# Quarter sums on GpSimd ahead of the convolution, and the convolution's norm among V's tiles

## Chip, core and metric

The kernel runs on one core of one Trainium2 chip. What counts is the device time of one execution in microseconds. The core has five engines with a queue each: PE (TensorE, matmuls), DVE (VectorE), ACT (ScalarE), POOL (GpSimd) and SP (SyncE, which here only issues DMAs; POOL issues some too). Each takes its instructions in a fixed order and waits on semaphores for the others.

## What is computed

One layer of a streaming encoder over 1040 tokens (16 learned ones and 1024 of input) of width 1024: three token mixers on the normalised input, gated, added and projected, and then a hierarchical mixture of experts. Cut to what matters here:

```python
def conv_module(bv, bg, conv_w, conv_b, ln_g, ln_b):
    glu = bv * jax.nn.sigmoid(bg)
    y = causal depthwise convolution of glu with 31 taps, 256 channels
    y = layer_norm(y + conv_b, ln_g, ln_b)      # (y - mu) * rsqrt(var + EPS)
    return jax.nn.silu(y)

def mixer_layer(u, w_in, ...):
    a, bv, bg, q, k, v, fg, gates = split(u @ w_in)
    ya = pool_mixer(a, ...) @ w_out_a
    yb = conv_module(bv, bg, ...) @ w_out_b
    logf = jax.nn.log_sigmoid(fg + b_forget)
    yc = forgetting_attention(heads(q), heads(k), heads(v), logf) @ w_out_c
    g = jax.nn.sigmoid(gates)                   # three branches of 1024 each
    return (g[0] * ya + g[1] * yb + g[2] * yc) @ w_o
```

## The kernel before

**Precision.** Matmuls work on values that are split in two: a rounded part ("hi", made by ACT, L171) and the remainder ("lo", made by DVE or POOL as raw minus hi, L172). A product is three matmuls: hi by hi, hi by lo, lo by hi. The normalised input u lies transposed in four slots, hi and lo for each half of its channels (`u4`); `uq(part, r, c)` is a quarter of the real tokens' part of it: channel half r, token half c, 128 partitions x 4 x 512 = 128x2048 values.

**Order of the work.** The projections are jobs that run one after another on PE: the convolution's gate and value, the pool mixer's input, then K (four jobs, matmuls L177, evictions L290 and L291 into a ring of eight buffers, copies to DRAM by POOL's queue at L292 and L293), V (nine tiles of 128 tokens, two halves each, matmuls L587; a tile's values are split from PSUM, L171 and L172, into the same slot as K's ring, and copied to DRAM at L595), the forget gate (L605 to L627), and two jobs of Q. V's weights come in four blocks of 128x1040, each split on ACT and DVE.

The vector work of the mixers doesn't stand in jobs. `start_b` fills a list, `pending`, in the order pool mixer, convolution, sums; each job takes some entries from its head when it is emitted (`pump(n)`): 13 for each K job, 3 for each tile of V, 4 for each Q job, and all that is left (`pump(1000)`) at the start of `seven`. The convolution's entries are 62 taps on DVE (L455, L457: accumulator plus input times weight, 128x1024 each), then its norm: `ln_sum` and `ln_mean` (mean over channels by PE with a matrix of ones, L471, and DVE, L484), `ln_var` (variance, square root on ACT at L497, reciprocal on DVE at L498, one Newton step L499 to L502), `ln_out` for each half (L506 to L510), `ln_free`, and the spill of yb to DRAM (`dy`), which frees its slot.

**Sums and products.** The rest of Q and the three gates, 13 column pairs, are computed in `seven` by seven half-size products for each pair instead of eight (a scheme of Strassen's kind; L680, 1092 matmuls of 512 columns). Its right sides are quarters of u and four sums of quarters: x = u01 - u00 (kept in place of u01 at the end, L639, L640), `tq[3]` = u11 - u01, `tq[2]` = u11 - x, `tq[4]` = u10 - tq[2]'s sum, each added over its hi and lo parts in two scratch halves x and y of slot `s_wx`, and split again (L545, L546). Its left sides are sums of weight blocks, made by POOL (L659 to L662) in the halves of the same slot `s_wx`, then split. The results go to DRAM as `dq` and `dg`. Attention, the projections out and the experts follow.

Within a stage the order of the instructions on each engine is set when the program is built: by the order of the code, as far as what an instruction needs is ready by then.

Of the kernel before, what the change touches and what calls it, by code (L numbers as in the profile page):

```python
# [8 lines left out]
F32R = mybir.dt.float32r  # L9
BF16 = mybir.dt.bfloat16  # L10
I32 = mybir.dt.int32
AF = mybir.ActivationFunctionType
# [29 lines left out]
def view(a, off, shape, dt=None):  # L42

    n = 1
    for s in shape:
        n *= s
    a = a[:, off:off + n]
    if dt is not None:
        a = a.bitcast(dt)
    if len(shape) == 2:  # L50
        a = a.rearrange("p (a b) -> p a b", b=shape[1])
    elif len(shape) == 3:
        a = a.rearrange("p (a b c) -> p a b c", b=shape[1], c=shape[2])
    return a
# [63 lines left out]
def f32(ap):  # L118
    return ap.bitcast(F32)


def body(tc, A, out):
# [3 lines left out]
    with es:  # L126
# [171 lines left out]
        def pump(n):  # L298
            for _ in range(min(n, len(pending))):
                pending.pop(0)()  # L300
# [91 lines left out]
        def start_b(_):  # L392
            s_x.free(), s_un.free()
            nonlocal qk_r
            s_qk, s_acc, s_ya = sl.take(F32R), sl.take(), sl.take(F32R)
            st["s_qk"], st["s_acc"], st["s_ya"] = s_qk, s_acc, s_ya
            qk_r = s_qk.ring(512, 8)
            st["acc"], st["sq"] = s_acc.new([2, S]), s_acc.new([2, S])
            st["yaT"] = s_ya.new([2, 2, S])
            queue_pool()  # L400
            queue_conv()
            queue_sums()

        job(lambda: None, start_b)

# [42 lines left out]
        def queue_conv():  # L448
            acc = st["acc"]

            def tap(k, ct):
                src = glu[:, ct, k:k + S]
                wk = cvec[:, 31 * ct + k:31 * ct + k + 1]
                if k == 0:
                    ve.tensor_scalar(acc[:, ct, :], src, wk, vec("conv_b", ct), ALU.mult, ALU.add)  # L455
                else:
                    ve.scalar_tensor_tensor(acc[:, ct, :], src, wk, acc[:, ct, :], ALU.mult, ALU.add)  # L457
            for k in range(31):
                for ct in range(2):
                    pending.append(lambda k=k, ct=ct: tap(k, ct))  # L460

            def both(x, ct):

                yb = st["ybT"]
                t = st["sq"][:, ct, :]
                ve.tensor_add(t, x[:, 0, :], x[:, 1, :])
                split(t, yb[:, 0, ct, :], yb[:, 1, ct, :])

            def over_channels(o, ct, cs):
                for part in range(2):  # L470
                    pe.matmul(o, ones, st["ybT"][:, part, ct, cs], start=part == 0, stop=part == 1)  # L471

            def ln_sum():
                st["s_yb"] = sl.take(F32R)
                st["ybT"] = st["s_yb"].new([2, 2, S])
                both(acc, 0)

            def ln_mean():
                for c in range(2):
                    o = mm_bk.next()  # L480
                    cs = slice(c * 512, c * 512 + 512)
                    over_channels(o, 0, cs)
                    for ct in range(2):
                        ve.scalar_tensor_tensor(acc[:, ct, cs], o, -1.0 / 256, acc[:, ct, cs], ALU.mult, ALU.add)  # L484
                        ac.activation(st["sq"][:, ct, cs], acc[:, ct, cs], AF.Square)

            def ln_var():
                vr, rs = sg_r.next([L])[:, 0:S], sg_r.next([L])[:, 0:S]
                st["rs"] = rs
                both(st["sq"], 1)  # L490
                for c in range(2):
                    o = mm_bk.next()
                    cs = slice(c * 512, c * 512 + 512)
                    over_channels(o, 1, cs)
                    ve.tensor_scalar(vr[:, cs], o, 1.0 / 256, EPS, ALU.mult, ALU.add)

                ac.activation(rs, vr, AF.Sqrt)  # L497
                ve.reciprocal(rs, rs)  # L498
                ve.tensor_mul(vr, vr, rs)  # L499
                ve.tensor_mul(vr, vr, rs)  # L500
                ve.tensor_scalar(vr, vr, -0.5, 1.5, ALU.mult, ALU.add)
                ve.tensor_mul(rs, rs, vr)  # L502

            def ln_out(ct):
                z, sq = acc[:, ct, :], st["sq"][:, ct, :]
                ve.tensor_mul(z, z, st["rs"])  # L506
                ve.tensor_scalar(z, z, vec("conv_ln_g", ct), vec("conv_ln_b", ct), ALU.mult, ALU.add)
                ac.activation(sq, z, AF.Sigmoid)
                ve.tensor_mul(sq, z, sq)
                yb = st["ybT"]  # L510
                split(sq, yb[:, 0, ct, :], yb[:, 1, ct, :])

            def ln_free():
                st["s_acc"].free(), s_glu.free()
            pending.extend([ln_sum, ln_mean, ln_var, lambda: ln_out(0), lambda: ln_out(1), ln_free,
                            lambda: spill(1, "yb")])

# [3 lines left out]
        def uq(part, r, c):  # L521
            return u4[2 * part + r][:, :, M + c * 512:M + c * 512 + 512]

        def queue_sums():
            def begin():
                st["s_t"] = [sl.take(F32R) for _ in range(3)]
                st["s_wx"] = sl.take()
                for n, x in zip((2, 3, 4), st["s_t"]):
                    tq[n] = [x.new([4, 512]) for _ in range(2)]
                st["x"], st["y"] = (view(st["s_wx"].ap, o, [4, 512]) for o in (2048, 0))  # L530
            pending.append(begin)

            def diff(to, r1, c1, r0, c0, other):

                return [lambda: ve.tensor_sub(st[to], f32(uq(0, r1, c1)), f32(uq(0, r0, c0))),
                        lambda: ve.tensor_sub(st[other], f32(uq(1, r1, c1)), f32(uq(1, r0, c0))),
                        lambda: ve.tensor_add(st[to], st[to], st[other])]

            def less(to, r, c, of):

                return [lambda: ve.tensor_sub(st[to], f32(uq(0, r, c)), st[of]),
                        lambda: ve.tensor_add(st[to], st[to], f32(uq(1, r, c)))]

            def parts(n, of):
                return [lambda: ac.copy(tq[n][0], st[of]),  # L545
                        lambda: ve.tensor_sub(tq[n][1], st[of], f32(tq[n][0]))]  # L546
            pending.extend(diff("x", 1, 1, 0, 1, "y") + parts(3, "x") + diff("x", 0, 1, 0, 0, "y") +
                           less("y", 1, 1, "x") + parts(2, "y") + less("y", 1, 0, "y") + parts(4, "y"))

        def qk_job(col, hp, which, n, look=2):  # L550
            def comp(w):
# [5 lines left out]
            job(lambda: win_unit(col + hp * P), comp, look)  # L557

        for hp in range(4):
            qk_job(COL_K, hp, 0, 13)  # L560


        def start_v(_):
# [9 lines left out]
        def v_all(ws):  # L573

            for j in range(9):
# [17 lines left out]
                        ve.tensor_add(st["lf"][:m, :, j], o[:, 252:260], bfb[:m, :])  # L593
                if j < 8:
                    gp.dma_start(dv[j * P:(j + 1) * P, :], f32(v.rearrange("p h t d -> p (h t d)")))  # L595
                pump(3)

        job(lambda: [win_unit(COL_V + half * 260, 260, k0, k0 + 4) for half in range(2) for k0 in (0, 4)], v_all, 1)

# [1143 lines left out]
```

## Time and profile before

| | us |
|---|---|
| device time, median of 3 runs | 1220.85 (1216.33 to 1223.65) |
| device time of the profiled execution | 1217.87 |
| its span | 1216.2 |
| PE busy in the span | 1059.8 (87%) |
| DVE busy | 804.1 (66%) |
| ACT busy | 517.2 (43%) |
| POOL busy | 398.2 (33%) |

PE is the engine to follow: where it is idle, the span grows. The page's slices show where in the span that is, and the timeline of PE, with what ended each idle time, shows what it waited for there. The rows of the other engines in the same stretch then show why the thing waited for was late.

### The profile page before, as it was taken

How to read it: one execution, taken by the hardware profiler on the slowest of the kernel's cores; microseconds unless marked ns; L12 is line 12 of the kernel's file. 1: busy time of each engine (PE TensorE's matmuls, PEld its weight loads, DVE VectorE, ACT ScalarE, POOL GpSimd, SP SyncE). 2: the span in 40 equal slices, each digit the busy share in tenths (PEclk: the TensorE clock that was granted, in tenths of full speed). 3: DMA queues.
4: the chain of work that ended last, by engine and by line, in shares of the span. 5: the costliest groups of instructions: out<-in, count | busy, mean ns of one | idle time of the engine just before them, and what ended most of it. 6: DMA issues, size and time to landing. Idle time of an engine off the chain costs nothing. (4 is left out here: it accounts for less than half of the span.)

```text
span 1216.2 us, 16197 instructions
## 1 busy us (share of the span) xinstructions
PE 1059.8 (87%) x5429; PEld 883.2 (73%) x5429; DVE 804.1 (66%) x1383; ACT 517.2 (43%) x943; POOL 398.2 (33%) x459
## 2 busy tenths in 40 slices
PE   5999999614999999998999999899976889889683
PEld 5999998413788888877888888777755667767562
DVE  5799956785443443326888885467778765567864
ACT  5312225222443444436888731222324544445552
POOL 4001210323333231112333138400015664454664
PEclk9999999856999999998999999999987899999995
DMA  7413522301423233187996557243557896696974
GB/s 216 119 54 116 181 97 95 143 0 34 156 87 122 97 120 114 60 251 191 243 300 141 197 158 235 102 157 139 179 192 232 284 322 184 164 301 175 293 244 150
DMA packets 95191, 202.10 MB, mean 166 GB/s; under 512 B 11730, under 2 KB 51747, under 8 KB 94549
## 3 DMA queue, kind: packets, MB, share of 16 engines
q1 hardware_dynamic: 83844, 167.83, 43.0%
q0 software_dynamic: 10784, 31.13, 9.1%
q10 hardware_dynamic: 432, 1.57, 0.4%
q8 instruction: 60, 0.98, 0.3%
q14 instruction: 71, 0.57, 0.1%
HBM read 148.94 MB, written 58.30 MB: 170 GB/s over the span
## 5 line engine op out<-in xcount | busy, mean ns | idle before, releaser
L680 PE MATMUL ps<-slot,slot 128*128 128x512 f32 x1092 | 264.0, 404 | 54.3 <-ACT slot L171 46.1
L172 DVE TENSOR_TENSOR slot<-slot,slot 128x512 fp32r<-128x512 f32 (+3 forms) x227 | 233.6, 1048 | 117.0 <-ACT slot L171 112.0
L680 PEld LDWEIGHTS ps<-slot,slot 128*128 128x128 f32 x1092 | 211.0, 194 | 106.6 <-ACT slot L171 47.1
L171 ACT CAST slot<-slot 128x512 fp32r<-128x512 f32 (+3 forms) x244 | 188.0, 797 | 218.4 <-PE ps L177 77.0
L177 PE MATMUL ps<-slot,slot 128*128 128x512 f32 (+3 forms) x1200 | 228.0, 350 | 2.1 <-ACT slot L251 1.2
L177 PEld LDWEIGHTS ps<-slot,slot 128*128 128x128 f32 x1200 | 204.1, 189 | 22.8 <-ACT slot L251 1.7
L1422 PE MATMUL ps<-slot,slot 128*128 128x512 f32 x552 | 141.0, 411 | 19.0 <-PEq L1704 10.5
L1422 PEld LDWEIGHTS ps<-slot,slot 128*128 128x128 f32 x552 | 107.7, 198 | 50.1 <-issue 16.8
L172 DVE TENSOR_TENSOR slot<-ps,slot 128x512 fp32r<-128x512 f32 (+6 forms) x166 | 84.8, 533 | 28.5 <-ACT slot L171 27.6
L1189 PE MATMUL ps<-slot,slot 128*128 128x512 f32 x384 | 99.5, 405 | 3.8 <-ACT slot L171 3.8
L177 PE MATMUL ps<-slot,sm 128*128 128x512 f32 x276 | 81.2, 443 | 24.2 <-DVE sm L1438 22.8
L171 ACT CAST slot<-ps 128x512 fp32r<-128x512 f32 (+6 forms) x166 | 74.3, 464 | 54.1 <-PE ps L587 27.5
L177 PEld LDWEIGHTS ps<-slot,sm 128*128 128x128 f32 x276 | 55.1, 210 | 40.4 <-DVE sm L1438 27.0
L1189 PEld LDWEIGHTS ps<-slot,slot 128*128 128x128 f32 x384 | 69.9, 191 | 16.7 <-ACT slot L171 3.9
L172 POOL TENSOR_TENSOR slot<-slot,slot 128x1024 fp32r<-128x1024 f32 x32 | 79.5, 2506 | 1.0 <-ACT slot L171 0.5
L457 DVE SCALAR_TENSOR_TENSOR slot<-slot,c,slot 128x1024 f32<-128x1024 f32 x60 | 75.3, 1280 | 0.5
L659 POOL TENSOR_TENSOR slot<-slot 128x512 f32<-128x512 f32 x13 | 18.7, 1437 | 166.5 <-DMA slot<-in_w_in_dram 126.1
L817 DVE CUSTOM_DVE_ANT_0 slot<-ps,slot 128x656 f32<-128x656 f32 (+7 forms) x64 | 49.3, 771 | 24.5 <-PE ps L812 17.5
L872 PE MATMUL ps<-const,slot 128*128 128x128 f32 x352 | 60.4, 283 | 1.5 <-DVE slot L172 1.2
L689 DVE TENSOR_TENSOR slot<-ps,slot 128x512 f32<-128x512 f32 x39 | 27.0, 691 | 51.6 <-PE ps L680 29.6
L947 POOL TENSOR_TENSOR slot<-slot,slot 128x512 f32<-128x512 f32 x32 | 47.3, 1502 | 38.3 <-DVE slot L946 32.8
L182 POOL TENSOR_SCALAR stats<-stats 128x1 f32<-128x1 f32 (+1 forms) x24 | 17.5, 728 | 115.2 <-ACT slot L181 114.4
(287 smaller groups left out, 1493.7 us busy)
## 6 DMA issues: line engine op xcount, KB each, us to landing
slot<-in_exp_w_dram SPq DMA_DIRECT2D x96, 512.0 KB
slot<-in_w_in_dram SPq DMA_DIRECT2D x13, 1024.0 KB
dg<-slot SPq DMA_DIRECT2D x48, 256.0 KB
slot<-dk SPq DMA_DIRECT2D x32, 260.0 KB
slot<-in_x_dram SPq DMA_DIRECT2D x16, 512.0 KB
slot<-dg SPq DMA_DIRECT2D x16, 512.0 KB
slot<-in_w_in_dram SPq DMA_DIRECT2D x12, 512.0 KB
slot<-dF SPq DMA_DIRECT2D x8, 520.0 KB
```

What stands on the lines that cost most here:

```text
L171: ac.copy(hi, raw)
L172: (lo_eng or ve).tensor_sub(lo, raw, f32(hi))
L177: pe.matmul(o, a, b, start=i == 0, stop=i == len(ops) - 1)
L457: ve.scalar_tensor_tensor(acc[:, ct, :], src, wk, acc[:, ct, :], ALU.mult, ALU.add)
L659: gp.tensor_sub(s3, a[0, 0], a[1, 0])
L680: pe.matmul(o, x[:, k, :], y[:, k, :], start=i == 0 and m in (1, 2, 7), stop=i == 11 and m in (2, 3, 4), skip_group_check=True)
L689: ve.tensor_add(t, bank(n, m), t)
L817: ve.tensor_tensor_reduce(out=s2, in0=o, in1=n2, scale=-1.0, scalar=3.0e38, op0=ALU.add, op1=ALU.min, accum_out=mn)
L872: pe.transpose(tp[:, t * P:(t + 1) * P], p_of(g, i0 + t)[:, b * P:(b + 1) * P], ident)
L947: gp.tensor_add(m, m, t)
L1189: pe.matmul(o[:, c, :], a, b, start=n == 0, stop=n == 23)
L1422: pe.matmul(o, x[:, k, :], wk, start=q == 0 and i == 0, stop=q == 1 and i == len(ops) - 1)
```

## The change

The two first sums of quarters, x and y = tq[2]'s sum, leave the end of the list: they become five POOL operations in one entry ahead of the convolution, in a slot of their own (`s_wx` is taken there). What is left of the sums is two entries at the end of the list: `two` (splits for tq[2] and tq[4], with the two DVE sums between them) and `third` (tq[3], three DVE sums and its split), and only `third` takes the slot that yb's spill gives free. The norm's root is exp(-0.5 ln(var)) by two table functions on ACT in place of a square root on ACT and a reciprocal on DVE. Each K job takes 20 entries instead of 13, so that all entries up to `ln_var` are emitted by the end of K, and V's tiles 3 to 8 take 1, 1, 1, 2, 2 and 2: `ln_out` twice, `ln_free`, the spill with `two`, and `third`.

```diff
             queue_pool()
+            queue_sums()
             queue_conv()
-            queue_sums()
+            queue_parts()
...
-                ac.activation(rs, vr, AF.Sqrt)
-                ve.reciprocal(rs, rs)
+                ac.activation(rs, vr, AF.Ln)
+                ac.activation(rs, rs, AF.Exp, scale=-0.5)
                 ve.tensor_mul(vr, vr, rs)
...
         def queue_sums():
-            def begin():
-                st["s_t"] = [sl.take(F32R) for _ in range(3)]
+
+            def sums():
                 st["s_wx"] = sl.take()
-                for n, x in zip((2, 3, 4), st["s_t"]):
+                x, y = st["x"], st["y"] = [view(st["s_wx"].ap, o, [4, 512]) for o in (2048, 0)]
+                gp.tensor_sub(x, f32(uq(0, 0, 1)), f32(uq(0, 0, 0)))
+                gp.tensor_sub(y, f32(uq(1, 0, 1)), f32(uq(1, 0, 0)))
+                gp.tensor_add(x, x, y)
+                gp.tensor_sub(y, f32(uq(0, 1, 1)), x)
+                gp.tensor_add(y, y, f32(uq(1, 1, 1)))
+            pending.append(sums)
+
+        def queue_parts():
+            def two():
+                st["s_t"] = [sl.take(F32R) for _ in range(2)]
+                for n, x in zip((2, 4), st["s_t"]):
                     tq[n] = [x.new([4, 512]) for _ in range(2)]
...
-            pending.extend(diff("x", 1, 1, 0, 1, "y") + parts(3, "x") + diff("x", 0, 1, 0, 0, "y") +
-                           less("y", 1, 1, "x") + parts(2, "y") + less("y", 1, 0, "y") + parts(4, "y"))
+                y = st["y"]
+                for n in (2, 4):
+                    ac.copy(tq[n][0], y)
+                    ve.tensor_sub(tq[n][1], y, f32(tq[n][0]))
+                    if n == 2:
+                        ve.tensor_sub(y, f32(uq(0, 1, 0)), y)
+                        ve.tensor_add(y, y, f32(uq(1, 1, 0)))
+
+            def third():
+
+                st["s_t"].append(sl.take(F32R))
+                tq[3] = [st["s_t"][2].new([4, 512]) for _ in range(2)]
+                y = st["y"]
+                ve.tensor_sub(y, f32(uq(0, 1, 1)), f32(uq(0, 0, 1)))
+                ve.tensor_add(y, y, f32(uq(1, 1, 1)))
+                ve.tensor_sub(y, y, f32(uq(1, 0, 1)))
+                ac.copy(tq[3][0], y)
+                ve.tensor_sub(tq[3][1], y, f32(tq[3][0]))
+            pending.extend([two, third])
...
-            qk_job(COL_K, hp, 0, 13)
+            qk_job(COL_K, hp, 0, 20)
...
-                pump(3)
+                pump({3: 1, 4: 1, 5: 1, 6: 2, 7: 2, 8: 2}.get(j, 0))
```

Line numbers of the changed kernel are one higher up to the norm (L457 is L458) and twelve higher behind the sums (L587 is L599, L680 is L692).

On POOL, in the stretch of the second K job, the difference of the two orders reads so. `dk` is K in DRAM, slots 93 to 96 are the four slots of u (93 and 94 hi, 95 and 96 lo), slot 866 is `s_wx`:

```order
+L292 DMA dk<-slot_749 128x400
+L530 TENSOR_TENSOR slot_866<-slot_93 128x2048
+L531 TENSOR_TENSOR slot_866<-slot_95 128x2048
+L293 DMA dk<-slot_749 128x400
+L532 TENSOR_TENSOR slot_866<-slot_866 128x2048
+L292 DMA dk<-slot_749 128x384
+L533 TENSOR_TENSOR slot_866<-slot_94,slot_866 128x2048
+L293 DMA dk<-slot_749 128x384
+L534 TENSOR_TENSOR slot_866<-slot_866,slot_96 128x2048
 L292 DMA dk<-slot_749 128x256
 L293 DMA dk<-slot_749 128x256
```

The five sums stand between the copies of one K job, which followed one another without anything between them before.

On DVE, at the end of K and the start of V, the order before. Slot 750 is the convolution's accumulator, slot 97 its input, slots 90 to 92 are a weight block, raw, hi and lo, slot 749 is K's ring and V's buffers:

```order
L457 SCALAR_TENSOR_TENSOR slot_750<-slot_97,c_2_75,slot_750 128x1024 x3
L291 SCALAR_TENSOR_TENSOR slot_749<-ps,slot_749 128x384
L457 SCALAR_TENSOR_TENSOR slot_750<-slot_97,c_2_75,slot_750 128x1024
L291 SCALAR_TENSOR_TENSOR slot_749<-ps,slot_749 128x256
L172 TENSOR_TENSOR slot_92<-slot_90,slot_91 128x1040
L457 SCALAR_TENSOR_TENSOR slot_750<-slot_97,c_2_75,slot_750 128x1024 x2
L172 TENSOR_TENSOR slot_749<-ps,slot_749 128x4x64
```

And now:

```order
L458 SCALAR_TENSOR_TENSOR slot_750<-slot_97,c_2_75,slot_750 128x1024 x2
L291 SCALAR_TENSOR_TENSOR slot_749<-ps,slot_749 128x256
L458 SCALAR_TENSOR_TENSOR slot_750<-slot_97,c_2_75,slot_750 128x1024 x3
L172 TENSOR_TENSOR slot_92<-slot_90,slot_91 128x1040
L458 SCALAR_TENSOR_TENSOR slot_750<-slot_97,c_2_75,slot_750 128x1024
L172 TENSOR_TENSOR slot_92<-slot_90,slot_91 128x1040
L458 SCALAR_TENSOR_TENSOR slot_750<-slot_97,c_2_75,slot_750 128x1024
L172 TENSOR_TENSOR slot_92<-slot_90,slot_91 128x1040
L458 SCALAR_TENSOR_TENSOR slot_750<-slot_97,c_2_75,slot_750 128x1024
L172 TENSOR_TENSOR slot_92<-slot_90,slot_91 128x1040
```

V's four weight splits stood apart among K's evictions, one of them the one shown; now all four stand behind K's last eviction, with taps between them.

Further on, DVE's order around the sums, before, where the products (L689, L700) have begun:

```order
L700 SCALAR_TENSOR_TENSOR slot_749<-slot_749 128x512
L535 TENSOR_TENSOR slot_1907<-slot_94,slot_93 128x2048
L536 TENSOR_TENSOR slot_1907<-slot_96,slot_95 128x2048
L537 TENSOR_TENSOR slot_1907<-slot_1907 128x2048
L536 TENSOR_TENSOR slot_1907<-slot_95 128x2048
L546 TENSOR_TENSOR slot_1905<-slot_1907,slot_1905 128x2048
```

And now, in V's last tiles (slot 1655 takes the split of `tq[2]`):

```order
L545 TENSOR_TENSOR slot_1655<-slot_866,slot_1655 128x2048
L172 TENSOR_TENSOR slot_749<-ps,slot_749 128x4
L172 TENSOR_TENSOR slot_749<-ps,slot_749 128x3x64
L605 TENSOR_TENSOR sm_23_1234<-ps,c_2_75 128x8
L547 TENSOR_TENSOR slot_866<-slot_94,slot_866 128x2048
L172 TENSOR_TENSOR slot_749<-ps,slot_749 128x4x64
L548 TENSOR_TENSOR slot_866<-slot_866,slot_96 128x2048
```

The splits and sums of the parts moved from behind Q's evictions to between the evictions of V's tiles. On SP the spill of yb now stands ahead of the second pair's weights, and at the end of the products a load of the first branch (L868, 128x4x1024, 2 MB) ahead of the first head's loads of q and k.

## Rows read from the trace of the kernel before

**Rows 1.** The page: TensorE's busy tenths in 40 slices of the span, and DRAM traffic.

```profile
PE   5999999614999999998999999899976889889683
...
HBM read 148.94 MB, written 58.30 MB: 170 GB/s over the span
```

**Rows 2.** Timeline of TensorE: start, duration, line, operands, count, idle before and releaser.

```profile
144.56 51.59 PE L587 MATMUL ps<-slot,slot 128*128 128x260 f32 x432
195.99 1.09 PE L471 MATMUL ps<-slot,ones 128*128 128x512 f32 x4
197.93 5.58 PE L177 MATMUL ps<-slot,slot 128*128 128x512 f32 x23 [0.85 <-DVE sm L593]
...
222.09 2.02 PE L680 MATMUL ps<-slot,slot 128*128 128x512 f32 x8
225.94 8.32 PE L680 MATMUL ps<-slot,slot 128*128 128x512 f32 x28 [1.83 <-DVE slot L291]
266.09 5.33 PE L680 MATMUL ps<-slot,slot 128*128 128x512 f32 x12 [31.82 <-ACT slot L171]
285.71 9.66 PE L680 MATMUL ps<-slot,slot 128*128 128x512 f32 x29 [14.30 <-ACT slot L171]
299.99 18.21 PE L680 MATMUL ps<-slot,slot 128*128 128x512 f32 x67 [4.62 <-ACT slot L685]
319.25 214.26 PE L680 MATMUL ps<-slot,slot 128*128 128x512 f32 x924 [1.04 <-ACT slot L685]
...
540.21 0.39 PE L680 MATMUL ps<-slot,slot 128*128 128x512 f32 x1
```

**Rows 3.** Busy time by stretch: length, PE, PEld, DVE, ACT, POOL, granted clock, DMA.

```profile
50.00:145.00 95.00, 95.00 (x590) 92.86 (x589) 94.18 (x93) 19.86 (x34) 12.40 (x23) 1.00 0.33 107
145.00:196.00 51.00, 51.00 (x431) 49.85 (x430) 28.29 (x59) 12.17 (x38) 5.35 (x10) 1.00 0.30 113
...
222.00:300.00 78.00, 25.43 (x80) 18.83 (x78) 52.23 (x37) 21.30 (x24) 25.59 (x37) 0.64 0.17 59
...
330.00:540.00 210.00, 209.32 (x905) 169.44 (x904) 77.62 (x101) 85.25 (x145) 53.43 (x49) 1.00 0.36 117
```

**Rows 4.** Timelines of VectorE and ScalarE around the norm's root and the sums.

```profile
209.07 6.54 DVE L498 RECIPROCAL slot<-slot 128x1024 f32<-128x1024 f32 x1
...
241.53 2.29 DVE L535 TENSOR_TENSOR slot<-slot,slot 128x2048 f32<-128x2048 f32 x1 [6.83 <-DMA dy<-slot]
...
281.38 2.29 DVE L546 TENSOR_TENSOR slot<-slot,slot 128x2048 fp32r<-128x2048 f32 x1 [1.96 <-ACT slot L545]
...
205.35 1.28 ACT L497 ACT_TABLE_LOAD   x1
```

**Rows 5.** Timeline of VectorE in K: the pool mixer's last op, V's last weight split.

```profile
116.07 0.69 DVE L172 TENSOR_TENSOR slot<-slot,slot 128x512 fp32r<-128x512 f32 x1
...
145.55 1.23 DVE L172 TENSOR_TENSOR slot<-slot,slot 128x1040 fp32r<-128x1040 f32 x1
```

**Rows 6.** Timeline of GpSimd: two of the products' left sums, undisturbed.

```profile
265.35 1.26 POOL L660 TENSOR_TENSOR slot<-slot 128x512 f32<-128x512 f32 x1
266.69 1.61 POOL L661 TENSOR_TENSOR slot<-slot,slot 128x512 f32<-128x512 f32 x1
```

**Rows 7.** Timelines of VectorE and GpSimd where both work on SBUF, and one undisturbed row.

```profile
12.68 1.29 DVE L239 SCALAR_TENSOR_TENSOR slot<-slot,stats,slot 128x1024 f32<-128x1024 f32 x1 [0.79 <-POOL stats L183]
...
14.73 3.37 DVE L239 SCALAR_TENSOR_TENSOR slot<-slot,stats,slot 128x1024 f32<-128x1024 f32 x1 [0.70 <-POOL stats L183]
...
14.66 2.35 POOL L172 TENSOR_TENSOR slot<-slot,slot 128x1024 fp32r<-128x1024 f32 x1
...
994.23 9.03 DVE L172 TENSOR_TENSOR slot<-slot,slot 128x1024 fp32r<-128x1024 f32 x4
...
995.27 5.77 POOL L172 TENSOR_TENSOR slot<-slot,slot 128x1024 fp32r<-128x1024 f32 x2
...
1019.85 4.63 DVE L172 TENSOR_TENSOR slot<-slot,slot 128x1024 fp32r<-128x1024 f32 x4
```

**Rows 8.** Timeline of SyncE's DMA queue: the first load for attention's first head.

```profile
529.82 0.53 SPq L773 DMA_DIRECT2D slot<-dq  x1
```

More of the change, by code (lines that the diff above doesn't have):

```diff
@@ L524, in queue_sums @@
         def queue_sums():
-            def begin():
-                st["s_t"] = [sl.take(F32R) for _ in range(3)]
+            def sums():
                 st["s_wx"] = sl.take()
-                for n, x in zip((2, 3, 4), st["s_t"]):
-                    tq[n] = [x.new([4, 512]) for _ in range(2)]
[L530 to L546, printed above, removed]
-            pending.extend(diff("x", 1, 1, 0, 1, "y") + parts(3, "x") + diff("x", 0, 1, 0, 0, "y") +
-                           less("y", 1, 1, "x") + parts(2, "y") + less("y", 1, 0, "y") + parts(4, "y"))
+                x, y = st["x"], st["y"] = [view(st["s_wx"].ap, o, [4, 512]) for o in (2048, 0)]
```

## Prediction

> **What bounds the kernel now.** I read the summary first. TensorE's 40 slices stand at 8 to 9 tenths nearly everywhere, and there is one hole: the eighth to tenth slices show 6, 1 and 4 [rows 1]. Then TensorE's timeline from the projections to the products tells what the hole is [rows 2]. V's 432 matmuls run from 144.56 to 196.15 without a break, Q's run to 222.1, and the first products (L680) start there. From then to 319 the row of L680 is cut up by idle times of 1.83, 31.82, 14.30, 4.62 and 1.04 us, 53.6 us in sum, and after 319.25 the products run on with hardly a break (924 in 214.26 us, 0.232 us each). All 1092 at that pace would take 253.2 us; they take from 222.1 to 540.6, that is 318.5. So 65 us are lost: 53.6 idle, the rest because the pieces between the gaps run at a granted clock that averages 0.64 from 222 to 300, where it is 1.00 from 330 to 540 [rows 3].
>
> What is late in the hole is read from VectorE's rows [rows 4]. Its reciprocal of the convolution's norm (L498) takes 6.54 us at 209. Then it waits 6.83 us for the spill of yb (DMA dy) because the sums need that slot, and from 241.53 to 283.7 it works through the sums of the quarters, one op of 2.29 us after another. ACT's casts and GpSimd's L659 stand behind these, and TensorE behind the casts. In V, on the other hand, VectorE is busy for only 28.29 of 51 us, ACT for 12.17 and GpSimd for 5.35 [rows 3]. That is the room that the change wants to use.
>
> **The change, part by part.** *What goes from VectorE behind V.* Five sums of 2.29 us go to GpSimd (11.5 us) and the reciprocal becomes two passes on ACT (6.5 us): 18.0 us less for VectorE. What is left of norm and parts (three splits, five sums) is handed out among V's tiles by the order, and the wait for the spill is gone, since x and y get a slot that is free early and only the third part waits for one more. ACT pays two passes over the norm and a table load ahead of each (1.28 us as at L497 [rows 4]), some 5 us in a stretch where it idles 38.8 us: nothing on the path. So if V's end and Q's end stayed, products would start at 222 with their parts ready, and up to 65 us would come back.
>
> *What it costs ahead of V.* The five GpSimd sums become free to start when VectorE's last op on the pool mixer ends (116.07 + 0.69, rows 5). They fall into the convolution's taps, where VectorE has no gap to give (busy 94.18 of the 95 us from 50 to 145 [rows 3]). A GpSimd sum over 128x512 takes 1.26 us and one over two slots 1.61 [rows 6]; four times these give 5.0 and 6.4 for 128x2048. I take 5.0, since three of the five have both inputs in one slot as the 1.26 row does, and keep 6.4 as the bound.
>
> They don't run beside the taps. At 14.73 an op of VectorE with two inputs in SBUF took 3.37 us where the one before took 1.29: it ended one such duration after GpSimd's op of 14.66 + 2.35. At 994.23 four took 9.03 us beside two GpSimd ops of 5.77, where four undisturbed ones took 4.63 [rows 7]. So VectorE lost 4.4 us, nearly the 4.7 us (2 x 2.35) that the two GpSimd ops need alone. The Trainium skill has the rule for it (SBUF — State Buffer, section "SBUF: two separate sides"): the port pair that VectorE and GpSimd share is an exclusive lock for the whole instruction, taken by a VectorE op with two SBUF inputs against a GpSimd op that reads SBUF, and the loser blocks. By that rule moving work from VectorE to GpSimd while VectorE runs such ops saves VectorE nothing, which speaks against this half of the change; the trace agrees, with 4.4 of 4.7 us lost.
>
> A tap (L457) has two SBUF inputs, so each sum holds VectorE for its 5.0 us, and between two sums one tap passes: sums at 116.8, 122.9, 129, 135.1 and 141.2, the last ending at 146.2, VectorE some 24.5 us behind (32 with 6.4 each). Two of K's copies to DRAM (L292, L293) stand between sums on GpSimd's queue; they are late by up to the sum ahead of them, but so is VectorE, which needs their buffers again.
>
> *What queues behind that.* K's last eviction on VectorE, the op ahead of the split at 145.55 [rows 5], so comes at about 169.5. V's four weight splits (L172 128x1040) were spread through K before, the last ending at 146.8; now they stand behind K's evictions and three taps, with a tap between each two. Four splits of 1.2 and six taps of 1.2 from 169.5 give 181.8 for the last. TensorE finishes K at 144.6 as before, can do 32 matmuls of V's first two tiles on the rounded parts alone as PSUM banks come free, and then waits. After the last split it finishes these two tiles at about 186.5, some of it at the lower clock, as behind the gap of 31.82 us (12 matmuls in 5.33 us, 0.44 each, [rows 2]); in the trace they were done at 156.0 (144.56 + 2 tiles of 5.72). V is 30 us late, and that is one new gap of TensorE of some 25 us.
>
> *From there on.* Seven tiles more: 336 matmuls of 0.119 us (51.59 / 432) are 40.1, the norm's eight matmuls 2.2, (four take 1.09 at 195.99), so V ends at 229. VectorE has the norm and the parts to do among them, by its order done at about 243; GpSimd then makes the first pair's left sums (four ops, 5.7 us) by 249. Q is 24.2 us as before (197.9 to 222.1): 253. I add 2 us for hand-overs between the engines around the forget gate, as the idle 0.85 us ahead of Q at 197.93 is one. The products start at 255 instead of 222.1, and go through at 0.232 us: 255 + 253.2 + 2 for small waits = 510 instead of 540.6. That is 30 us. Behind them the order sets a 2 MB load of the branch (L868) ahead of the first head's loads on SP's queue. No row of the trace shows that order. At 170 GB/s, the span's mean [rows 1], 2 MB are 12 us of transfer; the head's loads are issued from 529.8 [rows 8], 10.8 us ahead of the last product's end, so the cost lies between nothing and some 5 us, and I take 2. Sum: 1217.9 - 30 + 2 = 1190 against the profiled execution. The median of the runs shown is 3.0 above that execution, so 1193.
>
> **Rivals.** *No lock for these sums (0.13).* The sums run beside the taps and VectorE isn't held. For it: the rows of the lock are of L172 and L239, none has a tap. Then GpSimd's queue binds instead: K's copies stand behind sums, VectorE waits some 8 us for a ring buffer, the splits are still at the back, V is 13 us late, products start at 238 and end at 493: a gain of 47 - 2, 1173 (1176 by the median).
>
> *The lock holds and is dearer, or VectorE becomes the bound through V and Q (0.14).* Sums of 6.4 put all of it 7.5 us later; parts that are finished after 255 leave TensorE waiting at the first products, as in the trace. Either gives back 7 to 18 us: 1200 to 1211.
>
> *Slower than before (0.04).* One mechanism: the length of a GpSimd sum. All that V is late by comes from five times that length; the gain of 28 is gone when each holds the port 5.6 us longer, that is at 10.6 us. Row by row nothing is near it: the longest GpSimd op of 128x512 that wasn't held up is 1.61 [rows 6], 6.4 for four. At 12 us it would be 1228.
>
> *The change doesn't do what it says (0.02).* The norm and the parts could still stand behind V. The order excludes that for the norm; it would be same as before plus the late V, and lies within the last case. A wait of SP for the early spill of yb delays only the second pair's raw load, which is wanted some 20 us after the first product.
>
> **How the numbers follow.** The likeliest case (0.67) gives 1193, with 1186 to 1200 of its own. The range takes in the most of both neighbours: 1175 without the lock, 1210 with longer sums or a VectorE that is late. A measurement of this kernel can tell about 0.5%, 6 us, from no change, so the bounds are 1215 and 1227. Faster: the likeliest case, the first two rivals less a little: 0.91. Within: what lies between a gain of 6 and a loss of 6, 0.05. Slower: 0.04.
>
> **What the profile of the changed kernel would show.** Five GpSimd rows of L530 to L534 at about 117 to 146, of 5 us each, and beside them taps of about 6 us where 1.28 is usual; if the taps stay at 1.28, the first rival is right. V's last 128x1040 split near 182; a gap of TensorE of about 25 us in 145 to 185, and a granted clock below 1 behind it. No wait of VectorE for DMA dy of 6.8 us. L680 from about 255 to 510 with no idle time above 2 us; a gap there of 5 us or more on ACT's casts speaks for the second rival. Two table loads at L498 and L499, with nobody waiting. I would be wrong altogether if TensorE's gap before V were above 53 us, for then the same loss has only changed its place.

## The result and the profile after

The changed kernel takes 1190.24 us (median of 4 runs, 1188.46 to 1193.37) where the kernel before takes 1219.87 beside it: a ratio of 0.9759, 95% interval 0.9723 to 0.9796, some 29 us or 2.4% faster. The forecast was 1193, in 1175 to 1210. The profiled execution took 1189.95 us with a span (first to last instruction) of 1188.2, 28.0 shorter than before.

TensorE's busy tenths by slice show that the hole of [rows 1] is gone, and that a shallower one stands ahead of where it was (the fifth and sixth slices, 8 and 5, where 9 and 9 stood):

```profile
PE   5999859999999999979999999899957889989783
```

TensorE's timeline tells the same by stage: start, duration, line, count, idle before and its releaser. L599 is V, L177 K and then Q, L692 the products, L823 attention's scores:

```profile
109.63 34.73 PE L177 MATMUL ps<-slot,slot 128*128 128x400 f32 x216
155.73 2.10 PE L599 MATMUL ps<-slot,slot 128*128 128x260 f32 x8 [11.38 <-DVE slot L291]
...
171.31 2.10 PE L599 MATMUL ps<-slot,slot 128*128 128x260 f32 x8 [2.64 <-DVE slot L172]
...
193.00 30.97 PE L599 MATMUL ps<-slot,slot 128*128 128x260 f32 x258
223.80 17.09 PE L177 MATMUL ps<-slot,slot 128*128 128x512 f32 x73
...
250.86 79.41 PE L692 MATMUL ps<-slot,slot 128*128 128x512 f32 x342
...
499.11 5.86 PE L692 MATMUL ps<-slot,slot 128*128 128x512 f32 x24 [0.67 <-ACT slot L697]
508.52 0.72 PE L823 MATMUL ps<-slot 128*128 128x264 f32 x3 [3.56 <-DMA slot<-dk]
```

Set beside [rows 2]: V begins with waits for VectorE and ends at 223.97 where it ended at 196.15; Q moves with it; the products start at 250.86 instead of 222.09, but go through in 254.1 us instead of 318.5, with no idle time above 0.7 us. They end at 504.97 instead of 540.60, 35.6 us earlier. Behind them 7.6 us are given back: attention begins with a wait of 3.56 us for the first head's k, where the scores stood among the last products before.

The stretches show where the waiting went (length, PE, PEld, DVE, ACT, POOL, granted clock, DMA share, GB/s). VectorE is now full in V, 47.11 of 51 us against 28.29 in [rows 3], TensorE is busy for 32.84 of them at a granted clock of 0.73 (0.50 from 155.7 to 174, behind the idle 11.38 us: the lower of its two levels, 1.2 GHz), and from 222 to 300 the clock is 0.98 where it was 0.64:

```profile
145.00:196.00 51.00, 32.84 (x207) 30.47 (x208) 47.11 (x59) 11.34 (x25) 8.03 (x15) 0.73 0.32 107
...
222.00:300.00 78.00, 75.58 (x331) 61.14 (x330) 52.53 (x74) 37.78 (x59) 36.67 (x58) 0.98 0.40 130
```

The five sums on GpSimd, and VectorE's taps (L458) beside them, each tap in a window of its own, from the two engines' timelines:

```profile
116.53 4.63 POOL L530 TENSOR_TENSOR slot<-slot 128x2048 f32<-128x2048 f32 x1 [0.60 <-DVE slot L172]
121.12 5.62 POOL L531 TENSOR_TENSOR slot<-slot 128x2048 f32<-128x2048 f32 x1
...
127.27 5.03 POOL L532 TENSOR_TENSOR slot<-slot 128x2048 f32<-128x2048 f32 x1
...
132.82 5.03 POOL L533 TENSOR_TENSOR slot<-slot,slot 128x2048 f32<-128x2048 f32 x1
...
138.38 5.03 POOL L534 TENSOR_TENSOR slot<-slot,slot 128x2048 f32<-128x2048 f32 x1
...
116.78 5.46 DVE L458 SCALAR_TENSOR_TENSOR slot<-slot,c,slot 128x1024 f32<-128x1024 f32 x1
122.17 5.66 DVE L458 SCALAR_TENSOR_TENSOR slot<-slot,c,slot 128x1024 f32<-128x1024 f32 x1
127.75 5.64 DVE L458 SCALAR_TENSOR_TENSOR slot<-slot,c,slot 128x1024 f32<-128x1024 f32 x1
133.31 0.55 DVE L291 SCALAR_TENSOR_TENSOR slot<-ps,slot 128x384 fp32r<-128x384 f32 x1
133.77 5.17 DVE L458 SCALAR_TENSOR_TENSOR slot<-slot,c,slot 128x1024 f32<-128x1024 f32 x1
138.86 5.63 DVE L458 SCALAR_TENSOR_TENSOR slot<-slot,c,slot 128x1024 f32<-128x1024 f32 x1
...
166.10 0.42 DVE L291 SCALAR_TENSOR_TENSOR slot<-ps,slot 128x256 fp32r<-128x256 f32 x1
...
177.06 1.24 DVE L172 TENSOR_TENSOR slot<-slot,slot 128x1040 fp32r<-128x1040 f32 x1
```

Each of the five taps takes 5.17 to 5.66 us where one takes 1.28, and ends 1.1 us behind the end of a sum: sums and taps take turns, one tap for each sum. K's last eviction on VectorE comes at 166.10. Before the change it was at 145.20, in a profile where all of K lies 0.37 us later (TensorE's row of 109.63 stands at 110.00 there):

```profile
145.20 0.42 DVE L291 SCALAR_TENSOR_TENSOR slot<-ps,slot 128x256 fp32r<-128x256 f32 x1
```

So VectorE is 21.3 us behind. V's last weight split ends at 178.30.

### The profile page after: what moved, and what is told of

Same layout as the page of the kernel before. It is cut to its first block, busy times and chain, and to the rows that moved or that the text cites. A ratio compares the mean times of both kernels' runs of the same rounds, so it can differ in the third digit from the quotient of the medians.

```text
span 1188.2 us, 16197 instructions
## 1 busy us (share of the span) xinstructions
PE 1062.6 (89%) x5429; PEld 886.9 (75%) x5429; DVE 808.3 (68%) x1377; ACT 515.4 (43%) x944; POOL 417.5 (35%) x464
## 5 line engine op out<-in xcount | busy, mean ns | idle before, releaser
L692 PE MATMUL ps<-slot,slot 128*128 128x512 f32 x1092 | 253.4, 394 | 0.7 <-ACT slot L697 0.7
L692 PEld LDWEIGHTS ps<-slot,slot 128*128 128x128 f32 x1092 | 205.3, 188 | 48.6 <-ACT slot L697 1.1
L177 PE MATMUL ps<-slot,slot 128*128 128x512 f32 (+3 forms) x1200 | 228.8, 352 | 1.2 <-ACT slot L251 1.2
L177 PEld LDWEIGHTS ps<-slot,slot 128*128 128x128 f32 x1200 | 205.0, 189 | 22.0 <-ACT slot L251 1.7
L1434 PE MATMUL ps<-slot,slot 128*128 128x512 f32 x552 | 143.0, 416 | 19.5 <-PEq L1716 10.0
L1201 PE MATMUL ps<-slot,slot 128*128 128x512 f32 x384 | 100.6, 408 | 3.8 <-ACT slot L171 3.8
L177 PE MATMUL ps<-slot,sm 128*128 128x512 f32 x276 | 81.5, 445 | 23.7 <-DVE sm L1450 22.3
L458 DVE SCALAR_TENSOR_TENSOR slot<-slot,c,slot 128x1024 f32<-128x1024 f32 x60 | 96.0, 1632 | 0.5
L177 PEld LDWEIGHTS ps<-slot,sm 128*128 128x128 f32 x276 | 55.5, 211 | 39.6 <-DVE sm L1450 26.2
L599 PE MATMUL ps<-slot,slot 128*128 128x260 f32 (+1 forms) x432 | 59.2, 299 | 18.8 <-DVE slot L291 15.9
L599 PEld LDWEIGHTS ps<-slot,slot 128*128 128x128 f32 (+1 forms) x432 | 55.9, 192 | 22.2 <-DVE slot L291 17.0
L701 DVE TENSOR_TENSOR slot<-ps,slot 128x512 f32<-128x512 f32 x39 | 26.9, 691 | 51.5 <-PE ps L692 33.7
L884 PE MATMUL ps<-const,slot 128*128 128x128 f32 x352 | 60.8, 284 | 0.3 <-DVE slot L172 0.2
```

The source lines that it names most:

```text
L177: pe.matmul(o, a, b, start=i == 0, stop=i == len(ops) - 1)
L599: pe.matmul(o, u, w, start=i == 0, stop=i == len(ops) - 1)
L692: pe.matmul(o, x[:, k, :], y[:, k, :], start=i == 0 and m in (1, 2, 7), stop=i == 11 and m in (2, 3, 4), skip_group_check=True)
L701: ve.tensor_add(t, bank(n, m), t)
L884: pe.transpose(tp[:, t * P:(t + 1) * P], p_of(g, i0 + t)[:, b * P:(b + 1) * P], ident)
L1201: pe.matmul(o[:, c, :], a, b, start=n == 0, stop=n == 23)
```

## Experiments

Theory: each GpSimd sum holds VectorE for its length, V starts late by that, and the gain comes from what no longer stands between Q and the products. The rivals: the sums run beside the taps and V is late for another reason; or VectorE has no room among V's tiles. Each version changes the changed kernel unless said otherwise.

**The sums on VectorE, at the same place.**

```diff
-                gp.tensor_sub(x, f32(uq(0, 0, 1)), f32(uq(0, 0, 0)))
+                ve.tensor_sub(x, f32(uq(0, 0, 1)), f32(uq(0, 0, 0)))
...
```

> The changed kernel, with its five early sums given to VectorE at the same place in the list. Theory (each GpSimd sum holds VectorE for its length): VectorE pays 5 x 2.29 = 11.5 us where the changed kernel's rows show it 21.3 late (its last eviction of K at 166.1 against 144.9), so V's last weight split comes about 10 us earlier than 178.3, the products start near 241 instead of 250.9, and the time is about 1180. Rival (the sums run beside the taps, V is late for another reason): VectorE does 11.5 us more ahead of V, and the time is 1200 or above.

Measured: 1181.45 us, ratio to the kernel before 0.9719 (0.969 to 0.9749). V's last split ended at 169.0, the products started at 241.55:

```profile
167.78 1.22 DVE L172 TENSOR_TENSOR slot<-slot,slot 128x1040 fp32r<-128x1040 f32 x1
...
241.55 247.57 PE L692 MATMUL ps<-slot,slot 128*128 128x512 f32 x1068
```

Five operations more on VectorE, and the products start 9.3 us earlier. The median is 9 us lower than the changed kernel's; the two intervals overlap a little, but each of the six runs (1174.89 to 1185.78) lies below each of the changed kernel's. A GpSimd sum costs VectorE more (21.3 us for five) than doing the sums itself (11.4).

**The sums on GpSimd twice.**

```diff
+                gp.tensor_sub(x, f32(uq(0, 0, 1)), f32(uq(0, 0, 0)))
+                ... (the same five again)
```

> The changed kernel with its five GpSimd sums done twice in a row (the second pass computes the same again). Theory: VectorE is held a second time, by about another 21 to 25 us; V, Q and the products move by that: about 1213, with a gap of TensorE before V of some 45 us in all. Rival (sums beside the taps): GpSimd has the room, so at most the copies of K behind them are later; 1190 to 1198.

Measured: 1211.82 us, ratio 0.9941 (0.9914 to 0.9967). TensorE's wait ahead of V grew from 11.38 to 31.80 us, and the products started at 271.77, 20.9 later:

```profile
176.65 2.10 PE L604 MATMUL ps<-slot,slot 128*128 128x260 f32 x8 [31.80 <-DVE slot L291]
...
271.77 247.57 PE L697 MATMUL ps<-slot,slot 128*128 128x512 f32 x1068
```

Both times and both starts of the products fall on the theory's numbers (TensorE's waits in V's first two tiles add up to 39.2 us, not 45), and the first rival is out: the hold is real and grows with the sums.

**The sums on VectorE, behind the norm.** The sums' entry moves between the convolution's and the parts' entries, and VectorE does them.

```diff
-            queue_sums()
             queue_conv()
+            queue_sums()
             queue_parts()
```

> The changed kernel with the five sums on VectorE and queued behind the norm, among V's tiles, so that none of the change's sums stands ahead of V; the norm's new root and the handing out stay. Theory: nothing holds VectorE in K, V's last split comes at about 157 (only the four splits at the back of the taps are left of the delay), V ends near 203; the norm and the parts take VectorE until 239.4 - 21.3 + 11.5 = 230, the first pair's left sums until 235, so VectorE and no longer V's late start sets the start of the products, near 236: about 1175. Rival (V's tiles have no room for the sums): evictions of V wait behind them, TensorE stands still inside V, and products start at 250 as in the changed kernel: 1190.

Measured: 1176.02 us, ratio 0.9649 (0.9614 to 0.9683). TensorE waits 2.01 and 1.12 us ahead of V's first tiles, V ends at 206, and the products start at 230.56:

```profile
150.82 1.23 PE L599 MATMUL ps<-slot,slot 128*128 128x260 f32 x8 [2.01 <-DVE slot L172]
153.17 11.96 PE L599 MATMUL ps<-slot,slot 128*128 128x260 f32 x75 [1.12 <-DVE slot L172]
...
205.91 22.43 PE L177 MATMUL ps<-slot,slot 128*128 128x512 f32 x96
...
230.56 10.18 PE L692 MATMUL ps<-slot,slot 128*128 128x512 f32 x36
244.26 0.30 PE L636 MATMUL ps<-const,sm 128*72 128x128 f32 x1 [3.52 <-DVE sm L634]
```

VectorE had room for the sums among V's tiles, if only just: V takes 61 us instead of 51.6, and VectorE is busy for 57 of them. So the handing out, with the new root in it, brings the whole gain, and the sums on GpSimd ahead of V take 14 us of it away again.

**The old root.**

```diff
-                ac.activation(rs, vr, AF.Ln)
-                ac.activation(rs, rs, AF.Exp, scale=-0.5)
+                ac.activation(rs, vr, AF.Sqrt)
+                ve.reciprocal(rs, rs)
```

> The changed kernel with the old root (Sqrt on ScalarE, RECIPROCAL on VectorE), all else as changed. Theory: 6.5 us more of VectorE between V's tiles against one table load and one pass less on ScalarE; the chain of norm and parts, which ended at 239.4, ends some 5 us later and the first products wait for it in part: 1192 to 1196. Rival (the root has slack there): 1190, no difference.

Measured: 1199.58 us, ratio 0.9822 (0.9777 to 0.9868). The median is 9.3 us above the changed kernel's, more than expected and more than the row itself, but one of the four runs took 1191.0 and the two intervals overlap:

```profile
197.06 6.55 DVE L499 RECIPROCAL slot<-slot 128x1024 f32<-128x1024 f32 x1 [2.04 <-ACT slot L498]
```

In the profiled execution, the longest of the four, the root has no slack: the products end at 511.3 instead of 505.0. That is 6.3 of the 11.5 us by which its span is longer than the changed kernel's; the other 5.2 are lost behind the products, and what those are was not followed.

**The branch's load held back.** Two copies of one column make the load wait for attention's own results.

```diff
             if n == 60:
+                for q in range(2):
+                    ve.tensor_copy(st["mg4"][q][:, 0, 0:1], on[:, 0, 0:1])
                 load_branches()
```

> The changed kernel with the load of the first branch (L868, 2 MB) held back until attention's later groups, by two small copies into its slots ahead of it. Theory: this load is why attention's first scores wait for the head's k (idle 3.56 us at 508.5, the loads issued from 492.9 landing 12 to 15 us later, where they took some 7 before); without it the scores begin among the last products, as before the change: 4 to 6 us less, 1185. Rival (the loads are late for another reason, as their issue): within 2 us of the changed kernel, 1190.

Measured: 1186.56 us, ratio 0.9745 (0.9726 to 0.9763), 3.7 below the changed kernel's median, with intervals that overlap. The scores do begin among the last products, but the next one waits 5.34 us, for VectorE, which waits for GpSimd's mask, which waits for the forget rows (dF):

```profile
512.98 0.70 PE L823 MATMUL ps<-slot 128*128 128x400 f32 x1 [5.34 <-DVE sm L829]
...
511.75 0.43 POOL L810 TENSOR_TENSOR slot<-slot,const 128x128 f32<-128x128 f32 x1 [3.91 <-DMA slot<-dF]
```

So the load was at most a part of it. What held the forget rows is taken up two versions below.

**V's weight splits early.** The last K job's 20 entries are emitted behind V's weight splits.

```diff
-            qk_job(COL_K, hp, 0, 20)
+            qk_job(COL_K, hp, 0, 20 if hp < 3 else 0)
...
             gp.memset(st["lf"], 0.0)
+            pump(20)
```

> The changed kernel with the last K job's 20 entries emitted behind V's weight splits, so that these stand among K's evictions on VectorE again and nine taps behind them. Theory: of V's delay some 11 us are the splits' place behind the taps; V's last split comes at about 167 instead of 178.3 and V ends some 10 us earlier, but the norm and the parts are as much work for VectorE as before and end at about 239 still, the first pair's left sums at 245; so VectorE takes over as the bound and the products start near 245, not 240: 1184. Rival (V's start alone sets the products' start): the full 11 us, 1179.

Measured: 1189.83 us, ratio 0.9767 (0.9744 to 0.9789): no gain, against the theory and its rival. The last split ended at 168.5, ten microseconds earlier, and V ended at 224.8 all the same:

```profile
167.31 1.22 DVE L172 TENSOR_TENSOR slot<-slot,slot 128x1040 fp32r<-128x1040 f32 x1
168.45 10.84 DVE L458 SCALAR_TENSOR_TENSOR slot<-slot,c,slot 128x1024 f32<-128x1024 f32 x9
179.22 0.41 DVE L172 TENSOR_TENSOR slot<-ps,slot 128x256 fp32r<-128x256 f32 x1
...
168.58 9.66 PE L600 MATMUL ps<-slot,slot 128*128 128x260 f32 x60 [2.78 <-DVE slot L172]
180.95 5.02 PE L600 MATMUL ps<-slot,slot 128*128 128x260 f32 x29 [2.70 <-DVE slot L172]
```

TensorE went on for 60 matmuls and then waited for the first eviction of V, which stands behind nine taps and came at 179.22, as before. It got no farther than two tiles, four PSUM banks: the norm's four results (its entries are emitted ahead of V) have the other four of the ring of eight.

**The norm's first entries in V's tiles 0 to 2,** on top of the version above, so that its banks are taken later.

```diff
-            pump(20)
+            pump(17)
...
-                pump({3: 1,
+                pump({0: 1, 1: 1, 2: 1, 3: 1,
```

> The version with V's weight splits early (1189.8, V's end at 224.6), with the norm's three first entries emitted in V's tiles 0 to 2 instead of ahead of V. The norm's four PSUM banks are then not all taken from the ring ahead of V's tiles, and V's first six half tiles (144 matmuls) can go through before the first eviction instead of four (96). Theory (V is held by VectorE's taps, which stand ahead of V's evictions, and by how many banks there are until then): V ends about 48 x 0.119 = 5.7 us earlier, at 219; VectorE's chain is as long as before, so of that 0 to 4 us show in the time: 1186 to 1190. Rival (something else holds V): V's end stays at 224.

Measured: 1186.81 us, ratio 0.9758 (0.9735 to 0.9781). TensorE waited until 168.69, the end of the last split, and then ran 108 matmuls without a wait, where it had stopped after 60:

```profile
168.69 15.49 PE L600 MATMUL ps<-slot,slot 128*128 128x260 f32 x108 [8.37 <-DVE slot L172]
...
193.83 27.99 PE L600 MATMUL ps<-slot,slot 128*128 128x260 f32 x234
```

V ended at 221.8, 3.0 us earlier and not 5.7; the time, 1186.81 against 1189.83, is within the noise. That the banks are one of the things that hold V is shown. That in the changed kernel the splits, the evictions behind the taps and the banks hold it to nearly the same time, so that taking one away gains little, fits these two runs; no run takes away the evictions' place alone.

**The parts' slots in their old order.** The forget rows of the first head are loaded at 505.00, when the products have ended; before, their slot came free in time for a load some 15 us ahead of that end. The rows of SyncE's queue before:

```profile
525.19 1.83 SPq L780 DMA_DIRECT2D slot<-dF  x2
527.98 0.45 SPq L773 DMA_DIRECT2D slot<-dq  x1
```

The code has the reason: behind product 6 of the last pair it frees the first two slots of a list. The list was tq[2], tq[3], tq[4], and is tq[2], tq[4], tq[3] now that the third part is taken last; tq[4] is read by the very last product.

```diff
-                st["s_t"].append(sl.take(F32R))
-                tq[3] = [st["s_t"][2].new([4, 512]) for _ in range(2)]
+                st["s_t"].insert(1, sl.take(F32R))
+                tq[3] = [st["s_t"][1].new([4, 512]) for _ in range(2)]
```

> The changed kernel with the list of the parts' slots in its old order (tq[2], tq[3], tq[4]); nothing else. After the last pair's second product the kernel frees the first two of that list for attention's scores and forget rows; the change lists them as tq[2], tq[4], tq[3], and tq[4] is read by the very last product. Theory: that is why the first head's forget rows (dF) are loaded at 505.0, after the products, where they were loaded 15 us before the products' end, and why the branch's 2 MB load went ahead of the head's: with the right slots the scores begin among the last products again, 5 to 7 us less: 1184. It should gain more than holding back the 2 MB load did (3.7). Rival (the 2 MB load is the cause): as that version, 1187, or nothing.

Measured: 1186.53 us, ratio 0.9758 (0.974 to 0.9776). SyncE's queue in the changed kernel, and in this version:

```profile
490.14 0.37 SPq L868 DMA_DIRECT2D slot<-dg  x1
492.90 0.45 SPq L785 DMA_DIRECT2D slot<-dq  x1
...
505.00 0.80 SPq L792 DMA_DIRECT2D slot<-dF  x2
```

```profile
490.58 1.25 SPq L792 DMA_DIRECT2D slot<-dF  x2
493.34 0.45 SPq L785 DMA_DIRECT2D slot<-dq  x1
```

The forget rows are back ahead of the head's loads, the 2 MB load has gone behind them by itself, and the second block of scores waits 0.23 us:

```profile
506.53 0.45 PE L823 MATMUL ps<-slot 128*128 128x400 f32 x1 [0.23 <-DVE sm L829]
```

From the products' end to the output projection's first matmul it is 240.7 us (505.8 to 746.5) where the changed kernel takes 246.3 (505.0 to 751.3) and the kernel before took 241.6. So the mechanism is shown in the trace. How much of it is a gain of the whole is less sure:

> The changed kernel itself, unchanged, to set it beside the version with the right slots (1186.5, ratio to the kernel before 0.9758, interval 0.974 to 0.9776) in runs of the same hours. If the slots' gain, 5.6 us between the products' end and the output projection's first matmul in the two traces, is a gain of the whole, this kernel's ratio lies near 0.980 (1191 beside 1216); if it is lost again later, near 0.976 (1187).

Measured: 1189.98 us, ratio 0.9779 (0.9753 to 0.9805). The medians lie 3.5 us apart and the intervals overlap; between nothing and 5.6 us is what can be said.

**Sums behind the norm and splits early.**

> The version with the sums on VectorE behind the norm, and V's weight splits early as well. Theory: V is no longer late at all (ends near 197), but VectorE's chain of norm, sums and parts was the bound in the version without the early splits and is no shorter: products start near 229, TensorE stands still between Q and them for some 5 to 8 us: 1173 to 1177, no more than 3 us less. Rival (V's end was the bound there too): 8 to 9 us less, 1167.

Measured: 1175.59 us, ratio 0.9664 (0.9636 to 0.9691), as the version without the early splits. V ended at 203 and the products started at 225.18, but were cut up again until 267 by waits for VectorE's and ScalarE's work, 8.8 us in sum. VectorE is busy for 55 of V's 58 us and for all of Q's 22: it is the bound there.

**Sums on GpSimd behind the last tap,** with early splits. A copy of one column of the accumulator into each scratch half keeps the sums from starting earlier.

```diff
+                for t in (x, y):
+                    ve.tensor_copy(t[:, 0, 0:1], st["acc"][:, 1, 0:1])
                 gp.tensor_sub(x, f32(uq(0, 0, 1)), f32(uq(0, 0, 0)))
```

> Early weight splits, and the five sums on GpSimd but held behind the last tap by a copy of one column of the accumulator into each scratch half, so that they run beside V's evictions, whose inputs VectorE takes from PSUM. Theory: GpSimd holds VectorE only where the norm has two inputs in SBUF; VectorE is relieved of 11.5 us less what is lost to the port, some 5: the chain ends 5 to 7 us earlier than with the sums on VectorE, products start near 223: 1167 to 1171. Rival (the port takes it all back, as it did beside the taps): as with the sums on VectorE or later, 1175 or above.

Measured: 1181.95 us, ratio 0.9704 (0.9688 to 0.972): 6 us slower than the version above, with the sums on VectorE, and V ended at 215.4. The expectation was wrong by 11 us or more. VectorE, GpSimd and ScalarE in V's first tiles:

```profile
163.52 4.44 DVE L172 TENSOR_TENSOR slot<-slot,slot 128x1024 fp32r<-128x1024 f32 x1 [0.32 <-ACT slot L171]
...
168.56 2.49 DVE L484 SCALAR_TENSOR_TENSOR slot<-ps,slot 128x512 f32<-128x512 f32 x4 [0.18 <-PE ps L471]
...
178.24 5.85 DVE L172 TENSOR_TENSOR slot<-slot,slot 128x1024 fp32r<-128x1024 f32 x1 [0.39 <-ACT slot L171]
...
161.37 5.52 POOL L532 TENSOR_TENSOR slot<-slot 128x2048 f32<-128x2048 f32 x1 [14.20 <-DVE slot L531]
166.84 5.64 POOL L533 TENSOR_TENSOR slot<-slot 128x2048 f32<-128x2048 f32 x1
172.41 0.56 POOL L610 DMA_DIRECT2D dv<-slot  x1
...
176.51 0.76 ACT L171 CAST slot<-ps 128x256 fp32r<-128x256 f32 x3 [4.80 <-DMA dv<-slot]
```

Two things take the room back. Where the norm's split has two inputs in SBUF, VectorE is held: 4.44 and 5.85 us for what takes 1.22. And V's copies to DRAM (L610) queue behind the sums on GpSimd, so that ScalarE waits 4.80 us for a buffer of V's ring. That second one is the mechanism of the prediction's first rival, in another place. The four operations of L484 beside the sum of 166.84, with one input from PSUM, took 2.49 us as they do without one (2.48).

**Sums behind the norm, splits early, right slots.**

> The three findings together: sums on VectorE behind the norm, V's weight splits early, the right slots freed. Theory: the slots' gain adds to the 1175.6 of the first two, since it lies behind the products: 1169. Rival (attention's start is bound by VectorE's or the queue's order there): 1175.

Measured: 1173.12 us (1169.77 to 1173.47, 5 runs), ratio 0.9631 (0.9614 to 0.9647): the lowest median of all, 17 us below the changed kernel. It lies between the expectation and its rival; from the version without the right slots (1175.59) it is not told apart, since the intervals overlap.

## Why the prediction was right, step by step

- **The bound.** That the products' hole was VectorE's lateness between Q and the products held: with the norm and parts handed out, the products run 254.1 us in one piece, against 253.2 worked out from the pace after 319.25.
- **The lock.** The step that mattered most, since the change alone suggests that work on GpSimd is free. The sums took 4.63, 5.62 and three times 5.03 us (forecast 5.0), one tap passed between each two as forecast, and VectorE fell 21.3 us behind (forecast 24.5). The size was off by the price of one sum: 5.0 was taken, but only the first sum's row, 4.63, has no tap ahead of it, the others begin while a tap still runs, and the five taps were held for 3.9 to 4.4 us each, 21.2 in sum. The two versions that take the sums away from GpSimd and double them there show the cause.
- **V's late start.** The number came out (the last split at 178.3 against 181.8, V's end at 224 against 229), but the cause named for some 11 us of it failed: I put them on the four weight splits at the back of the taps. Early splits gained nothing. The gap of 25 us that the splits were to end came as 18.8 us in six pieces, and 15.9 of these waited for K's late evictions (L291), which hold PSUM banks, only 2.9 for the splits. V's first evictions stand behind the same taps, and the norm's four banks leave TensorE only two tiles to work ahead. Had I asked what else V needs by 180, the list would have been longer than one.
- **Q, forget gate and start of the products.** 250.86 against 255: the last split came 3.5 us early (VectorE's 21.3 instead of 24.5), V took 45.7 us from there and not 47.2, and the way from V's end to the products took 26.9 and not 26. The parts ended at 239.4 (forecast 243), the left sums at 247.4 (249).
- **Attention's start.** The term of 2 us was mis-sized and had the wrong cause. From the products' end to attention's first transposes (L884) it is 10.0 us where it was 3.7, and at the output projection's first matmul 4.7 us are lost. I had seen the 2 MB load in SyncE's order and not asked why it could stand there: the head's forget rows had lost their slot to the order of a list in the change. The row of [rows 8], 529.82, is not the first load of that head either: its forget rows went at 525.19 and q from 527.98.
- **The sum.** 35.6 us from the products against 30 forecast, 4.7 lost in attention against 2, and 2.9 lost behind the output projection's start, in which nothing of the change lies and which no run here explains. That the end is 28.0 against 28 is luck: 5.6 us more from the products and 5.6 us more lost behind them cancel.
- **The rivals.** No lock: out, by the doubled sums. Dearer lock or VectorE as the bound: not in the changed kernel, but it is what limits the faster versions. Slower: the sums are far from 10.6 us. The root was worth 9.3 us by the medians and 6.3 at the products' end, about the 6.5 of its row. That nobody would wait for its table functions failed by little: VectorE stands idle for 1.93 us for the second of them.

## What to carry to other kernels

Before work goes to an idle engine, look in the trace for rows where the two engines work side by side: if one grows by the other's length, the engine that gives the work away pays for it all the same, and loses time wherever it has no gap. Handing a chain of vector work out among the tiles of an earlier stage brought 42 us here (the new root with it), and the sums belonged into that same room, on VectorE. When the order of takes in a pool changes, follow every place that frees by position: a slot freed while its last reader is still to come makes no error, only a late start.

## What the runs showed of the hardware that was not expected

GpSimd and VectorE took turns where both had work waiting: between each two of GpSimd's sums exactly one tap passed VectorE, also where nothing stood between the sums on GpSimd's queue (L530 and L531). So only five taps and one eviction passed in the 28 us from 116.5 to 144.5. The row of a sum that begins while a tap still runs contains the wait for it: 5.62 and 5.03 us against 4.63. Held operations are those with two inputs in SBUF: taps of 1.28 us took 5.17 to 5.66 and splits of 1.22 took 4.44 and 5.85, while operations with an input in PSUM kept their time (2.49 for four; 0.55 for K's eviction at 133.31, beside L533). The Trainium skill's rule (SBUF — State Buffer, section "SBUF: two separate sides") has both halves of that, the lock for the whole instruction and the condition of two SBUF inputs, and the rows agree with it in both.
